# Shared pools, hand-ordered transposes and re-timed weight preparation between the mixer and the feed forward of a hybrid encoder layer

## The chip, the cores and the metric

The kernel runs on one core of one Trainium2 chip. The time is that of one execution on the device, in microseconds (us). A core has TensorE (PE, matrix products into PSUM), VectorE (DVE), ScalarE (ACT) and GpSimd (POOL) for elementwise work, and SyncE (SP), whose queue issues the transfers between DRAM and the on-chip memory SBUF.

## The reference

One layer (DEPTH = 1) over 2048 tokens of width 1024 in float32: windowed attention and a state space mixer in parallel, their outputs through w_out, then a feed forward of width 4096 with a squared relu.

```python
h = rms_norm(x, norm1[layer])
z = h @ w_in[layer]
...
att = windowed_gqa(q, k, v, q_gain[layer], k_gain[layer], sink[layer])
ssm = s5_mixer(u, lam_re[layer], ..., w_glu[layer])   # ends in gelu, then g_val * sigmoid(g_gate)
x = x + jnp.concatenate([att, ssm], axis=-1) @ w_out[layer]
h = rms_norm(x, norm2[layer])
x = x + jnp.square(jax.nn.relu(h @ w_ff1[layer])) @ w_ff2[layer]
```

## The kernel before

Every float32 number is split into an upper and a lower part of a format that TensorE takes, and each product is three matmuls (`mm3`, lines 85 to 89: upper by upper, upper by lower, lower by upper). So each operand needs a split: ScalarE copies the upper part, VectorE or GpSimd subtracts it for the lower part.

First come the input projection, the state space scan and attention (to about 680 us). What the change touches begins there.

The middle. `yprep` (line 836) loads the scan's output y in four quarters of tokens, four pieces each, applies the gelu and splits. `glu` (line 850) makes 96 matmuls per quarter into banks `pglu`, and the gate `sg` gives s in the tiles `sth` and `stl`. `load_split` brings the state space half of w_out in eight pieces through two buffers; GpSimd subtracts. `out_ssm` (line 1203) does per token tile of 128 two halves of 12 matmuls into `pos_` banks and VectorE adds x1 (the residual with attention's part, loaded from `x1_dr`). `norm2` (line 1228) takes the squares' sum on ScalarE, two scalar steps on VectorE, a power on GpSimd, and scales to h2 on VectorE.

The feed forward runs on 2 x 2 blocks with seven products instead of eight (PRODUCTS, numbered 1 to 7), so from each pair of token tiles seven operand pieces are made: four blocks b11, b21, b12, b22 and sums of them (t2, t3, t4 on GpSimd). They go to DRAM (`hc_dr`), are loaded back, transposed on TensorE (`trans`, banks `pth`), and split into `hb`. The tokens are done in two halves of 1024, tiles 0 to 7 first. For each half 16 blocks of `ff1_block` follow (32 in all, each 84 matmuls); a block's w1 is loaded two blocks ahead, summed (`left_w1`) and split (`split_w1`) one block ahead. The results f11, f12, f21, f22 and their sums s1 to s4 go to DRAM (`f_dr`). In block 16 the operands change to the second half of the tokens.

The second matrix runs over 8 chunks of w2 by 4 units of 256 tokens (32 units, each seven products of 12 matmuls). Each chunk's w2 is loaded as two pairs (`load_w2`), eight sums are made on VectorE (`right_w2`, lines 1460 to 1463) and 14 splits (`split_w2`); f pieces are loaded (`load_f`, four buffers) and split (`split_f`) a unit ahead. After each product VectorE adds the bank into `acc` (line 1541), which was loaded with x1.

A scheduler orders each engine's instructions from a model of when they are ready, so the order in the program is not that of the source; each engine then takes its own queue in order. Tiles are taken from pools; a pool that is opened where another one lay waits until that one's last use. With `tc.manual_schedule` an engine keeps the source's order.

## Time and profile before

| what | us |
|---|---|
| median of 3 runs | 2201.45 (2196.33 to 2203.27) |
| the profiled execution | 2200.2 |
| its span, first to last instruction | 2198.4 |
| TensorE busy | 2077.8 (95%) |
| VectorE, ScalarE, GpSimd busy | 67%, 46%, 27% |
| first matrix of the feed forward | about 907 to 1537 |
| second matrix | about 1553 to 2194 |

The page gives for each engine the time in which it worked. Where the engine that sets the time is busy nearly all along, one reads its idle time: when it lay, what released it, and at which clock it ran (the granted clock, as a share of the full rate).

### The profile page before, as it was taken

Reading aid. Unit: us, or ns where it says so; the run is one execution under the profiler, and the core shown is the slowest. Engines: PE = TensorE matmul, PEld = TensorE weight load, DVE = VectorE, ACT = ScalarE, POOL = GpSimd, SP = SyncE. Lnnn points to the kernel's source line nnn. Section 1 sums busy time; section 2 is a strip of 40 time slices with the busy share of each in tenths; the row PEclk is TensorE's granted clock in tenths of the full one; section 3 lists DMA queues with packets and bytes.
Section 4 is the critical chain, followed back from the end, with each engine's and each line's share of the span. In section 5 each row is a group of like instructions: output and inputs, shape, how many; then the busy total and the mean of one; then the engine's idle time right before and its main releaser. Section 6 shows DMA issues by size and latency. Waiting matters only on the chain.

```text
span 2198.4 us, 30479 instructions
## 1 busy us (share of the span) xinstructions
PE 2077.8 (95%) x10546; PEld 1706.7 (78%) x10546; DVE 1479.6 (67%) x2806; ACT 1016.0 (46%) x2061; POOL 590.3 (27%) x451
## 2 busy tenths in 40 slices
...
GB/s 252 292 82 159 157 125 142 108 100 117 96 125 160 163 153 279 224 149 152 153 158 176 203 156 146 146 151 99 255 212 101 129 128 98 134 130 114 112 135 162
DMA packets 284394, 337.06 MB, mean 153 GB/s; under 512 B 62928, under 2 KB 211408, under 8 KB 284240
## 3 DMA queue, kind: packets, MB, share of 16 engines
...
q8 instruction: 83, 1.36, 0.3%
q14 instruction: 71, 0.58, 0.1%
...
## 4 chain that ended last, share of the span: by engine, by line
PE 67%; DVE 13%; DMA 7%; POOL 5%; issue 3%; ACT 3%; SPq 1%; DVEq 0%; POOLq 0%; ACTq 0%
PE f L87 6%; PE f L89 6%; PE f L88 6%; PE f_al L89 5%; PE f_al L87 5%; PE f_al L88 5%; PE f_ga L87 3%; PE f_ga L89 3%; PE f_ga L88 3%; POOL w2s L1470 2%; PE pv L1075 1%; POOL fs L1496 1%; PE ptp L1065 1%; DVE acc L1541 1%; PE f_be L89 1%
## 5 line engine op out<-in xcount | busy, mean ns | idle before, releaser
L1541 DVE TENSOR_TENSOR acc<-f,acc 128x512 f32<-128x512 f32 x448 | 304.8, 687 | 164.6 <-PE f L89 158.0
L87 PE MATMUL f<-w2s,fs 128*128 128x512 f32 x896 | 352.9, 394 | 31.0 <-DVE acc L1541 15.7
L89 PE MATMUL f<-w2s,fs 128*128 128x512 f32 x896 | 351.4, 392 | 3.7 <-POOL fs L1496 3.7
L88 PE MATMUL f<-w2s,fs 128*128 128x512 f32 x896 | 351.3, 392 | 0.0
L1495 ACT ACTIVATE fs<-fr 128x512 fp32r<-128x512 f32 x224 | 141.6, 633 | 366.1 <-PE f L89 350.5
L1496 POOL TENSOR_TENSOR fs<-fr,fs 128x512 fp32r<-128x512 f32 x128 | 185.2, 1449 | 297.0 <-ACT fs L1495 255.8
L87 PEld LDWEIGHTS f<-w2s,fs 128*128 128x128 f32 x896 | 169.4, 189 | 74.1 <-ACT fs L1495 27.0
L1339 POOL TENSOR_TENSOR w1s<-w1r,w1s 128x512 fp32r<-128x512 f32 x96 | 135.2, 1409 | 311.9 <-ACT w1s L1338 303.0
L87 PE MATMUL f_al<-hb,w1s 128*128 128x512 f32 x512 | 201.0, 393 | 1.0 <-ACT w1s L1338 1.0
L89 PE MATMUL f_al<-hb,w1s 128*128 128x512 f32 x512 | 200.6, 392 | 1.1 <-DVE w1s L1339 0.9
L89 PEld LDWEIGHTS f<-w2s,fs 128*128 128x128 f32 x896 | 169.7, 189 | 40.3 <-POOL fs L1496 4.5
L88 PE MATMUL f_al<-hb,w1s 128*128 128x512 f32 x512 | 200.4, 391 | 0.0
L88 PEld LDWEIGHTS f<-w2s,fs 128*128 128x128 f32 x896 | 169.8, 190 | 34.7
L818 POOL TENSOR_TENSOR wgl<-wgr,wgh 128x512 fp32r<-128x512 f32 x8 | 10.4, 1311 | 521.0 <-DMA wgr<-in_w_glu_dram 508.2
L1339 DVE TENSOR_TENSOR w1s<-w1c,w1s 128x512 fp32r<-128x512 f32 x96 | 68.3, 711 | 88.0 <-ACT w1s L1338 88.0
L89 PEld LDWEIGHTS f_al<-hb,w1s 128*128 128x128 f32 x512 | 96.5, 189 | 22.0 <-DVE w1s L1339 1.3
L87 PEld LDWEIGHTS f_al<-hb,w1s 128*128 128x128 f32 x512 | 96.5, 189 | 21.3 <-ACT w1s L1338 1.4
L88 PEld LDWEIGHTS f_al<-hb,w1s 128*128 128x128 f32 x512 | 96.6, 189 | 19.6
L1338 ACT ACTIVATE w1s<-w1c 128x512 fp32r<-128x512 f32 x128 | 80.6, 630 | 49.7 <-PE f_al L89 48.4
L88 PE MATMUL f_ga<-hb,w1s 128*128 128x512 f32 x256 | 99.9, 390 | 0.0
L87 PE MATMUL f_ga<-hb,w1s 128*128 128x512 f32 x256 | 99.8, 390 | 0.0
L89 PE MATMUL f_ga<-hb,w1s 128*128 128x512 f32 x256 | 99.7, 389 | 0.0
...
## 6 DMA issues: line engine op xcount, KB each, us to landing
...
f_dr<-fs SPq DMA_DIRECT2D x128, 256.0 KB
...
```

What stands on the lines that cost most here:

```text
L87: nc.tensor.matmul(ps_ap, lhsT=lh, rhs=rh, start=first, stop=False, skip_group_check=onto)
L88: nc.tensor.matmul(ps_ap, lhsT=lh, rhs=rl, start=False, stop=False, skip_group_check=onto)
L89: nc.tensor.matmul(ps_ap, lhsT=ll, rhs=rh, start=False, stop=last, skip_group_check=onto)
L818: eng_lo.tensor_tensor(lo, raw, hi, op=ALU.subtract)
L1065: nc.tensor.transpose(pt[:, h, :], p[:, h, kt * P:(kt + 1) * P], ident)
L1075: nc.tensor.matmul(po[g * HD:(g + 1) * HD, :], lhsT=v_all[:, lo + kt, g * HD:(g + 1) * HD], rhs=pT.pop((n, g, kt)), start=kt == 0, stop=kt ...
L1338: ACT.activation(out=t[:, 0], in_=src, func=AF.Copy)
L1339: (DVE if m in (6, 7, 3) else POOL).tensor_tensor(t[:, 1], src, t[:, 0], op=SUB)
L1470: (DVE if m in (6, 7, 3) and fp else POOL).tensor_tensor(t[:, 1], src, t[:, 0], op=SUB)
L1495: ACT.activation(out=t[:, 0], in_=src, func=AF.Copy)
L1496: (DVE if m in (6, 7, 3) else POOL).tensor_tensor(t[:, 1], src, t[:, 0], op=SUB)
L1541: DVE.tensor_tensor(a[:, cs], po, a[:, cs], op=ADD)
```

## The change

Four things are changed.

1. One pool (`px0`, then `px`) stays open over both matrices of the feed forward. Its tiles `raw0` and `raw1` hold first s of the even quarters, then the raw w1 (both halves of a block in one tile), then the raw w2. Splits of w1, of w2 and of f share tags (`w0` to `w6`, pairs `fa` to `fd`, four `cp` cells). So the last ff1 block can prepare chunk 0 of w2 (loads, sums, 14 splits in part) and load four pieces of f. All small tiles are padded so that every tile begins at the same position modulo 256 bytes.
2. From token tile 8 to the first ff1 block TensorE's order is that of the source: `trans` reads h2, t2, t3, t4 directly from SBUF, two pieces after each half of `out_ssm`; tiles 8 to 15 don't pass through `hc_dr`. The first half of ff1 is now that of tiles 8 to 15; tiles 0 to 7 come through DRAM at the switch. t3 is now t2 - b11 (before: b22 less the old b12, GpSimd's), and from tile 8 on it is VectorE's.
3. The gelu of the next quarter and the loads of w_out are woven with the gate step by step, y pieces are loaded one ahead, and the first block's lower halves of w1 are all VectorE's, products 1 and 2 ahead of the sums.
4. In the second matrix each chunk's sums and splits stand at steps, one per product, instead of eight sums at two places. acc is not loaded: the first products of chunk 0 are copied into it by ScalarE (`FIRST_TO`), and x1 is added later by 32 additions on VectorE (`X_STEPS`, one buffer `x2`, tiles of w2's raw pair in the last chunk).

The core of the diff:

```diff
-    pos_stack, pn_stack, sb_stack = ExitStack(), ExitStack(), ExitStack()
+    pos_stack, pn_stack, px1_stack = ExitStack(), ExitStack(), ExitStack()
+
+    px0 = ctx.enter_context(tc.tile_pool(name="px0", bufs=1))
+    d1_stack, d1b_stack, pnb_stack = ExitStack(), ExitStack(), ExitStack()
     po_ = pos_stack.enter_context(tc.tile_pool(name="pos", bufs=1))
     wsh = po_.tile([P, 4, D], F32R, name="wsh")
     wsl = po_.tile([P, 4, D], F32R, name="wsl")
-    pn = pos_stack.enter_context(tc.tile_pool(name="pn", bufs=1))
-    g2 = pn.tile([P, D], F32, name="g2")
-    nc.sync.dma_start(out=g2, in_=norm2[0:1, :].to_broadcast([P, D]))
-    s_pools = [pos_stack.enter_context(tc.tile_pool(name="s1", bufs=1)),
-               sb_stack.enter_context(tc.tile_pool(name="s0", bufs=1))]
+    s_pool = pos_stack.enter_context(tc.tile_pool(name="s1", bufs=1))
...
+    def split_ws():
+        for half in range(2):
+            for k in range(4):
+                cs = slice(half * 512, half * 512 + 512)
+                load_split(pn, "x1", 2, w_out[0, AW + k * P:AW + (k + 1) * P, cs], wsh[:, k, cs], wsl[:, k, cs], POOL)
+                if k % 2:
+                    yield
...
-        pool = s_pools[(q + 1) % 2]
-        s_t[q] = tuple(pool.tile([P, 4, 512], F32R, tag=nm, name=nm) for nm in ("sth", "stl"))
+        pool, tags = (s_pool, ("sth", "stl")) if q % 2 else (px0, ("raw0", "raw1"))
+        s_t[q] = tuple(pool.tile([P, 4, 512], F32R, tag=tag, name=nm) for tag, nm in zip(tags, ("sth", "stl")))
...
-            junk = pn.tile([P, 512], F32, tag="junk", name="junk", bufs=1)
+            junk = ps.tile([P, 512], F32, tag="mm", name="junk")
...
-        POOL.tensor_tensor(t3, b22, b12, op=SUB)
-        POOL.tensor_tensor(b12, b12, b11, op=SUB)
-        POOL.tensor_tensor(t2, b22, b12, op=SUB)
+        first = n < NT // 2
+        if first:
+            for m, t in ((1, b11), (2, b21), (3, b22)):
+                nc.sync.dma_start(out=hc_dr[n // 2, m], in_=t)
+        eng = POOL if n < NT - 1 else DVE
+        eng.tensor_tensor(b12, b12, b11, op=SUB)
+        eng.tensor_tensor(t2, b22, b12, op=SUB)
+        (POOL if first else DVE).tensor_tensor(t3, t2, b11, op=SUB)
...
-    run(run_glu(0))
-    run(yprep(2), run_glu(1), out_quarter(0))
-    run(yprep(3), run_glu(2), out_quarter(1))
-    run(run_glu(3), out_quarter(2))
-    sb_stack.close()
+    weave(run_glu(0), yprep(1), split_ws())
+    weave(run_glu(1), yprep(2))
+    run(out_quarter(0))
+    weave(run_glu(2), yprep(3))
+    run(out_quarter(1))
+    pn_stack.close()
+    run(run_glu(3))
     glu_stack.close()
 
 
-    d1_stack = ExitStack()
+
     with tc.using_default_side("right"):
         pe = d1_stack.enter_context(tc.tile_pool(name="pe", bufs=1))
+        pn = pnb_stack.enter_context(tc.tile_pool(name="pnb", bufs=1))
+        px1 = px1_stack.enter_context(tc.tile_pool(name="px1", bufs=1))
+    g2 = load_gain(pn)
...
+    def raw_tile(i):
+        return px0.tile([P, 2, D], F32, tag=f"raw{i % 2}", name="wraw")
...
-    early = right_operands(0, [(m, i) for i in range(4) for m in PRODUCTS])
-    for n, _ in enumerate(out_quarter(3)):
-        if n > 0:
-            for _ in range(7):
-                next(early, None)
+    x1 = load_x1(NT // 2, px1, "x1", 2)
+
+    by_hand = ExitStack()
+    by_hand.enter_context(tc.manual_schedule(engines={mybir.EngineType.PE}))
+    queue = []
+    for n in range(NT // 2, NT):
+        nx = load_x1(n + 1, px1, "x1", 2) if n + 1 < NT else None
+        if n == NT - 1:
+            queue += [(m, 3, h2_t[n - 1][:, j * 512:j * 512 + 512]) for j, m in enumerate((1, 2))]
+        for _ in out_ssm(n, x1):
+            for _ in range(min(len(queue), 2 if n < NT - 1 else 3)):
+                trans(*queue.pop(0))
+        if n == 11:
+            load_w1(0)
+            load_w1(1)
+        nc.sync.dma_start(out=x1_dr[n * P:(n + 1) * P, :], in_=x1)
+        pend = norm2(n, x1)
+        if pend is not None and n < NT - 1:
+            queue += [(m, (n - NT // 2) // 2, pend[m]) for m in (1, 2, 3, 5, 6, 7, 4)]
+        x1 = nx
+    px1_stack.close()
     pos_stack.close()
...
+    px = ctx.enter_context(tc.tile_pool(name="px", bufs=1))
...
-        (DVE if m in (6, 7, 3) else POOL).tensor_tensor(t[:, 1], src, t[:, 0], op=SUB)
+        (DVE if m in (6, 7, 3) or g == 0 else POOL).tensor_tensor(t[:, 1], src, t[:, 0], op=SUB)
...
-        nc.sync.dma_start(out=f_dr[g % NFB, g // NFB, m], in_=t)
-
-    def cell(tag, bufs=1):
-        return pf.tile([P, 512], F32, tag=tag, name=tag, bufs=bufs)
+        nc.sync.dma_start(out=f_dr[g % NFB, 1 - g // NFB, m], in_=t)
...
+    def pair(tag):
+        t = px.tile([P, 2, 512], F32, tag=tag, name=tag)
+        return t[:, 0], t[:, 1]
...
-        f11 = cell("f11")
+        f11, f22 = pair("fa")
...
+    FS_PX = {1: "fa", 2: "fb", 7: "fc", 3: "fd"}
...
+    left_w1(0, (1, 2))
+    for m in (1, 2):
+        split_w1(0, m)
     left_w1(0)
...
+            k = PRODUCTS.index(m)
+            if k == 0:
+                right_w2(0, 0)
+            if k == 2:
+                right_w2(0, 1)
+            if k == 4:
+                load_f(0)
+                load_f(1)
+            if k == 5:
+                load_f(2)
+                load_f(3)
+                split_f(0)
+            for j in {1: (), 2: (1, 2)}.get(k, (k,)):
+                split_w2(0, j)
...
+    FIRST_TO = (1, 6, 5, 4)
...
+        steps = {3: load(0), 5: load(1)}
+        for fp in range(2):
+            for i, do in enumerate((sums, sum2, sum7, sum4)):
+                steps[11 + 4 * fp + i] = lambda do=do, fp=fp: do(fp)
+        for j in range(14):
+            steps[(14 if j < 4 else 17) + j, "split"] = lambda j=j: split_w2(c + 1, j)
+        return steps
...
+        for k in range(7):
+            if X_STEPS.get((u, k), (0, 1))[1] == 0:
+                n = X_STEPS[u, k][0]
+                if c < NC2 - 1:
+                    x2_t[n] = load_x1(n, p2, "x2", 1)
+                else:
+                    x2_t[n] = raw_tile(n)[:, 0]
+                    nc.sync.dma_start(out=x2_t[n], in_=x1_dr[n * P:(n + 1) * P, :])
...
-                DVE.tensor_tensor(a[:, cs], po, a[:, cs], op=ADD)
-            q = 7 * (u + 1) + k
-            split_f(q)
-            load_f(q + 4)
-            if more:
-                if u % 4 in (1, 2) and k == 3:
-                    right_w2(c + 1, u % 4 - 1)
-                if u % 4 == 3:
-                    for j in range(4 + 2 * k, min(6 + 2 * k, 14)):
-                        split_w2(c + 1, *W2_ORDER[j])
-                elif u % 4 == 2 and k > 2:
-                    split_w2(c + 1, *W2_ORDER[k - 3])
+                if c == 0 and m in FIRST_TO:
+                    ACT.copy(a[:, cs], po)
+                else:
+                    DVE.tensor_tensor(a[:, cs], po, a[:, cs], op=ADD)
+            if (u, k) in X_STEPS:
+                n, half = X_STEPS[u, k]
+                xs = slice(half * 512, half * 512 + 512)
+                DVE.tensor_tensor(acc[n][:, xs], acc[n][:, xs], x2_t[n][:, xs], op=ADD)
+            for q in F_STEPS[k] if u == 0 else (7 * (u + 1) + k,):
+                f_on(q)
+            if u == 0:
+                for j in W_STEPS.get(k, ()):
+                    split_w2(0, j)
+            step = 7 * (u % 4) + k
+            for do in (before.get((step + 28, "split")), plan.get(step), plan.get((step, "split"))):
+                if do is not None:
+                    do()
```

How the order moves, at three places. In the rows `[waits ...]` names the engines or queues whose signals the instruction waits for.

TensorE at the end of the middle, before; `pos_` is the out product of the last tile, `hs` a piece that comes from DRAM, `f_al` the first bank of ff1:

```order
L88 MATMUL pos__9407<-wsl,sth 128x512
L89 MATMUL pos__9407<-wsh,stl 128x512
L87 MATMUL pos__9407<-wsh,sth 128x512
L1292 MATMUL pth<-ident,hs 128x128 x4
L88 MATMUL pos__9407<-wsl,sth 128x512
L89 MATMUL pos__9407<-wsh,stl 128x512
L1292 MATMUL pth<-ident,hs 128x128 x72
L87 MATMUL f_al<-hb,w1s 128x512
```

After the change, in the last tile too; `t_9308`, `t_9307` and `t_9309` are t2, t3 and t4 of tiles 12 and 13 in SBUF:

```order
L92 MATMUL pos__9383<-wsh,sth 128x512
L93 MATMUL pos__9383<-wsl,sth 128x512
L94 MATMUL pos__9383<-wsh,stl 128x512
L1352 MATMUL pth<-ident,t_9308 128x128 x4
L1352 MATMUL pth<-ident,t_9307 128x128 x4
L1352 MATMUL pth<-ident,t_9309 128x128 x4
L92 MATMUL pos__9418<-wsh,sth 128x512
```

The 18 pieces that stood behind the last out product are now spread between the halves of the tiles, three here.

VectorE behind the last out product, before; L1294 is the lower half of a transposed piece, L1331 and L1329 are sums of w1, L1339 is the lower half of a product of w1:

```order
L1211 TENSOR_TENSOR x_9289<-pos__9407,x_9289 128x512 [waits PE_49]
L1235 TENSOR_TENSOR ss_9486<-ss_9486 128x1 [waits Activation_49]
L1236 TENSOR_SCALAR ss_9486<-ss_9486 128x1 [waits DVE_49]
L1238 SCALAR_TENSOR_TENSOR h_9485<-x_9289,ss_9486,g_7874 128x1024 [waits DMAHW1_49,DMAHW0_49,Pool_49]
L1294 TENSOR_TENSOR hb<-pth,hb 128x4x128 [waits Activation_49] x16
L1331 TENSOR_TENSOR w1c<-w1r 128x512 [waits DMAHW3_49,DMAHW2_49,DMAHW4_49,DMAHW1_49,DMAHW6_49,DMAHW0_49,DMAHW7_49,DVE_49,Pool_49]
L1294 TENSOR_TENSOR hb<-pth,hb 128x4x128 [waits Activation_49] x2
L1329 TENSOR_TENSOR w1c<-w1r 128x512 [waits DMAHW2_49]
L1339 TENSOR_TENSOR w1s<-w1c,w1s 128x512 [waits Activation_49]
L1330 TENSOR_TENSOR w1c<-w1c,w1r 128x512 [waits DVE_49]
```

After; L1354 is the lower half of a transposed piece, L1277 the scaling h2, L1290 to L1292 the sums of tiles 14 and 15, L1405 a sum of w1, L1415 a lower half of w1:

```order
L1248 TENSOR_TENSOR x_9314<-pos__9418,x_9314 128x512 [waits PE_49]
L1354 TENSOR_TENSOR hb<-pth,hb 128x4x128 [waits Activation_49] x2
L1274 TENSOR_TENSOR ss_9448<-ss_9448 128x1 [waits Activation_49]
L1275 TENSOR_SCALAR ss_9448<-ss_9448 128x1 [waits DVE_49]
L1277 SCALAR_TENSOR_TENSOR h_9447<-x_9314,ss_9448,g_8930 128x1024 [waits Pool_49]
L1290 TENSOR_TENSOR h_9447<-h_9447,h_9373 128x512 [waits DVE_49]
L1405 TENSOR_TENSOR wc<-wraw 128x512 [waits DMAHW5_49,DMAHW4_49]
L1291 TENSOR_TENSOR t_9458<-h_9447 128x512 [waits DVE_49]
L1415 TENSOR_TENSOR ws<-wraw,ws 128x512 [waits Activation_49]
L1292 TENSOR_TENSOR t_9457<-t_9458,h_9373 128x512 [waits DVE_49]
L1415 TENSOR_TENSOR ws<-wraw,ws 128x512 [waits Activation_49]
```

The lower halves of the first two products of w1 now stand between the sums of the last tile pair and ahead of the other sums of w1.

VectorE in the second matrix, at the turn of a chunk, before; L1541 adds a bank into acc, L1460 to L1463 are the sums of w2, L1496 is a lower half of f:

```order
L1496 TENSOR_TENSOR fs<-fr,fs 128x512 [waits DMAHW5_49,Activation_49]
L1460 TENSOR_TENSOR w2c<-w2r 128x512 [waits DMAHW6_49,DMAHW2_49,Pool_49]
L1541 TENSOR_TENSOR acc_15410<-f_16660,acc_15410 128x512 [waits PE_49]
L1461 TENSOR_TENSOR w2r<-w2r 128x512 [waits DVE_49]
L1541 TENSOR_TENSOR acc_15414<-f_16663,acc_15414 128x512 [waits PE_49]
L1496 TENSOR_TENSOR fs<-fr,fs 128x512 [waits DMAHW7_49,Activation_49]
L1541 TENSOR_TENSOR acc_15412<-f_16658,acc_15412 128x512 [waits PE_49]
L1462 TENSOR_TENSOR w2c<-w2r 128x512 [waits DVE_49]
L1541 TENSOR_TENSOR acc_15416<-f_16661,acc_15416 128x512 [waits PE_49]
L1463 TENSOR_TENSOR w2c<-w2r,w2c 128x512 [waits DVE_49,Pool_49]
L1541 TENSOR_TENSOR acc_14935<-f_16831,acc_14935 128x512 [waits PE_49]
```

After; L1736 adds into acc, L1660, L1667, L1672 and L1677 are the sums, L1558 is a lower half of f:

```order
L1558 TENSOR_TENSOR fs<-wc,fs 128x512 [waits DMAHW4_49,Activation_49]
L1660 TENSOR_TENSOR wraw<-wraw 128x512 [waits DMAHW7_49,Pool_49]
L1736 TENSOR_TENSOR acc<-f_16424,acc 128x512 [waits PE_49]
L1736 TENSOR_TENSOR acc<-f_16427,acc 128x512 [waits PE_49]
L1558 TENSOR_TENSOR fs<-wc,fs 128x512 [waits DMAHW5_49,Activation_49]
L1667 TENSOR_TENSOR wc<-wraw 128x512 [waits DMAHW1_49,DVE_49]
L1736 TENSOR_TENSOR acc<-f_16422,acc 128x512 [waits PE_49]
L1672 TENSOR_TENSOR wc<-wc,wraw 128x512 [waits DVE_49]
L1736 TENSOR_TENSOR acc<-f_16425,acc 128x512 [waits PE_49]
L1677 TENSOR_TENSOR wc<-wraw,wc 128x512 [waits Pool_49]
L1736 TENSOR_TENSOR acc<-f_16584,acc 128x512 [waits PE_49]
L1660 TENSOR_TENSOR wraw<-wraw 128x512 [waits DMAHW3_49]
```

The sum of b12 and b11 is now the first, the one that reads the second half of the raw tile comes two additions later, and behind them sums and additions alternate in both.

## Rows read from the trace of the kernel before

**Rows 1.** The page's part 1: engine, busy us (share of the span), number of instructions

```profile
PE 2077.8 (95%) x10546; PEld 1706.7 (78%) x10546; DVE 1479.6 (67%) x2806; ACT 1016.0 (46%) x2061; POOL 590.3 (27%) x451
```

**Rows 2.** Table by stretch: us, busy us of each engine, TensorE's clock, DMA share, GB/s

```profile
680.00:932.00 252.00, 223.37 (x958) 178.11 (x957) 140.52 (x196) 100.11 (x185) 73.97 (x63) 0.93 0.58 195
...
1240.00:1537.00 297.00, 297.00 (x1312) 245.93 (x1311) 146.53 (x208) 161.67 (x275) 79.62 (x59) 1.00 0.41 139
1537.00:1600.00 63.00, 39.15 (x141) 30.13 (x141) 44.71 (x49) 21.75 (x39) 35.65 (x25) 0.78 0.69 246
1600.00:2194.00 594.00, 583.14 (x2552) 477.28 (x2550) 424.71 (x588) 185.34 (x300) 283.42 (x192) 1.00 0.41 130
```

**Rows 3.** TensorE's waits, 680 to 932: for what, us in all, times, longest

```profile
PE pth L1292 <- DMA hs<-hc_dr: 12.1, 3, 6.7
...
PE pos__9119 L87 <- DVE x L1211: 3.9, 1, 3.9
PE pglu L87 <- ACT sg L862: 2.6, 1, 2.6
```

**Rows 4.** TensorE's timeline, 833 to 847: start, length, engine, line, operation, wait before

```profile
833.75 0.40 PE L88 MATMUL pos__9057<-wsl,sth 128*128 128x512 f32 x1
...
835.62 0.40 PE L87 MATMUL pos__9071<-wsh,sth 128*128 128x512 f32 x1
...
841.10 0.80 PE L87 MATMUL pos__9119<-wsh,sth 128*128 128x512 f32 x1 [3.92 <-DVE x L1211]
...
846.33 0.39 PE L87 MATMUL pos__9133<-wsh,sth 128*128 128x512 f32 x1
```

**Rows 5.** ScalarE's timeline, 699 to 710

```profile
699.09 0.63 ACT L817 ACTIVATE wsh<-x 128x512 fp32r<-128x512 f32 x1 [0.70 <-DMA x<-in_w_out_dram]
...
709.11 0.63 ACT L843 ACTIVATE y<-yr 128x512 f32<-128x512 f32 x1 [3.83 <-DMA yr<-y_dr]
```

**Rows 6.** VectorE's timeline around the scaling of a tile's norm

```profile
858.01 0.16 DVE L1235 TENSOR_TENSOR ss<-ss 128x1 f32<-128x1 f32 x1 [1.08 <-ACT junk L1234]
...
859.09 1.28 DVE L1238 SCALAR_TENSOR_TENSOR h<-x,ss,g 128x1024 f32<-128x1024 f32 x1 [0.73 <-POOL ss L1237]
```

**Rows 7.** GpSimd's timeline, one sum of transformed tokens

```profile
863.19 1.29 POOL L1251 TENSOR_TENSOR t<-h 128x512 f32<-128x512 f32 x1
```

**Rows 8.** TensorE's waits, 1537 to 2195

```profile
PE f L87 <- DVE acc L1541: 15.7, 15, 2.3
PE f L87 <- DMA fr<-f_dr: 15.3, 1, 15.3
PE f L89 <- POOL fs L1496: 3.7, 1, 3.7
```

**Rows 9.** TensorE's timeline at the boundary of the two matrices

```profile
1537.29 0.39 PE L89 MATMUL f_al<-hb,w1s 128*128 128x512 f32 x1
1552.92 0.80 PE L87 MATMUL f<-w2s,fs 128*128 128x512 f32 x1 [15.25 <-DMA fr<-f_dr]
```

**Rows 10.** VectorE's timeline in the second matrix

```profile
1643.73 0.87 DVE L1460 TENSOR_TENSOR w2c<-w2r 128x512 f32<-128x512 f32 x1 [2.09 <-POOL w2s L1470]
...
1645.12 1.18 DVE L1461 TENSOR_TENSOR w2r<-w2r 128x512 f32<-128x512 f32 x1
...
1657.01 0.68 DVE L1463 TENSOR_TENSOR w2c<-w2r,w2c 128x512 f32<-128x512 f32 x1
```

**Rows 11.** SyncE's queue, issue of one load of w2

```profile
1639.22 0.35 SPq L1453 DMA_DIRECT2D w2r<-in_w_ff_dram  x1
```

**Rows 12.** GpSimd's timeline before that load

```profile
1637.44 1.75 POOL L1470 TENSOR_TENSOR w2s<-w2r,w2s 128x512 fp32r<-128x512 f32 x1
```

**Rows 13.** TensorE's timeline, the stall after the sums

```profile
1652.16 0.47 PE L87 MATMUL f<-w2s,fs 128*128 128x512 f32 x1 [1.49 <-DVE acc L1541]
```

**Rows 14.** VectorE's timeline, the last s2 of the first matrix

```profile
1538.37 0.69 DVE L1394 TENSOR_TENSOR fs<-fs,f 128x512 f32<-128x512 f32 x1
```

**Rows 15.** Groups by line, GpSimd, 1600 to 2190: count, busy us, mean ns, idle before

```profile
L1496 POOL TENSOR_TENSOR fs<-fr,fs 128x512 fp32r<-128x512 f32 x118 | 171.0, 1451 | 289.1 <-ACT fs L1495 247.9 <-DVE acc L1541 41.2
```

314 lines of the change are left out of this document (200 added, 114 removed).

## The prediction

> **What bounds the kernel now.** I read the page's busy line first: TensorE is busy 2077.8 us of the 2198.4 us span [rows 1], so the change can only win what TensorE loses, and I looked for where that is. The table by stretch answers it [rows 2]. In the first feed forward matrix TensorE is busy 297.00 of 297 us at a granted clock of 1.00; nothing can be won there. Three stretches lose time. The middle, from attention's end to the first blocks of the feed forward (680 to 932), has 252 - 223.37 = 28.6 us idle, and its mean clock of 0.93 takes up to 0.07 x 252 = 17.6 us more: about 46. The boundary between the two feed forward matrices (1537 to 1600) has 23.9 us idle and a clock of 0.78, up to 13.9 more; since some of the slow clock falls into the idle time, I take 36. The second matrix (1600 to 2194) has 594 - 583.14 = 10.9 us idle at clock 1.00. Together about 93 us: the prize if every wait went and nothing came in its place. Then I asked the waits what ended these gaps. In the middle the longest are transposes that wait for pieces from DRAM (12.1 us), a sum that waits for x1 (3.9) and a gate (2.6) [rows 3]; at the boundary one wait of 15.3 us for the first f piece, one of 3.7 for POOL's split, the rest for VectorE's sums into acc [rows 8].
>
> **Middle: what goes, what comes.** The waits for DRAM pieces go: the transposes of tiles 8 to 15 read SBUF and stand between the two halves of each tile's product. The code gives no more transposes than before, and 28 loads and 28 stores of 256 KB less. I then walked through the new order with the old durations, and found these waits in it.
>
> First gate, quarter 0 to 1. The eight loads of w_out still go through two buffers, each held until POOL's split; the last lands at 699.09, and ScalarE then waited until 709.11 for the next y [rows 5]. In the new order ScalarE has the gelu of the last y piece of quarter 1 behind those splits, so it comes at about 710 to 711, while TensorE has used up quarter 0 and the pieces that are there at about 704. I put 6.7 us of idle plus 1.8 of slow clock: 8.5 (3 to 10).
>
> Tile 8. Its x1 and gain tiles lie in the place of the gate's pool, so their loads go out only after quarter 3's gate. In the trace a late x1 load made TensorE wait 3.92 us, and the 12 matmuls behind it took 846.33 - 841.10 = 5.2 us; at the spacing before it (835.62 - 833.75 = 1.87 us for 8, so 0.234 each) they would take 2.8 [rows 4]. So 3.9 + 2.4 = 6.3; I take 7, since here a gain load of the same size stands in the same queue (2 to 10).
>
> Tiles 9 to 13. The sum t3 is now VectorE's and waits for POOL's t2, which stands behind POOL's b12; each is about 1.3 us [rows 7], and two copies of transposed pieces are queued behind t3 on VectorE. TensorE needs their bank: 2 x 1.3 less 0.3 of other work, three times: 7 (0 to 9).
>
> Block 0. Behind tile 15 VectorE has, in a row, the two scalar steps, the scaling h2, then L1290, L1405, L1291, and only then the lower half of w1's first product. Scalar steps to the end of h2: 858.01 to 859.09 + 1.28 = 2.4 us, after 1.08 of waiting for the squares [rows 6]: 3.4; with four instructions at about 0.69 the half is there 6.2 us after the last sum, about 7 after the last product. TensorE has eight transposes (1 us), a wait for their copy (1.3) and two matmuls; the third needs that half: 4.3 idle, and about 2 of slow clock as in [rows 4]. With small change after it: 9 (6 to 11).
>
> Boundaries between quarters and leftovers: 3. Sum 8.5 + 7 + 7 + 9 + 3 = 34.5 against 46: **-12** (0 to -25).
>
> **Boundary of the two matrices.** The shared pool lets w2's loads, sums and first splits and four f loads run under the last ff1 block. What cannot move ahead of it: the first f split goes into the pair "fa", which f11 and f22 hold until the block's last s2 has read them. In the trace TensorE's last matmul starts at 1537.29 and the next at 1552.92 [rows 9]; s2 is done at 1538.37 + 0.69 = 1539.06 [rows 14], 1.4 us after TensorE's end. Then ScalarE's split and POOL's 1.45 us (mean of 118) [rows 15]: the first lower half is there about 3.5 to 4.5 us after the end, POOL's next some 3 us later. So 4.4 of idle and 2.5 of slow clock: 7 (5 to 12) in place of 36: **-29** (-24 to -31). The cover for w2's loads is the block's 19 us of matmuls; were it not enough, each missing load would cost the 4.5 us below.
>
> **The second matrix: the spread sums.** The stall that returns with every chunk of w2 is read at 1652.16: 1.49 us [rows 13]. VectorE's eight sums alternate with the additions into acc, 1.18 + 0.69 per addition, while TensorE brings one each 1.36 us, and it started late: the first sum at 1643.73 after 2.09 us of waiting [rows 10]. The page names POOL, but the load that the sum reads left at 1639.22 [rows 11], when POOL's split of the old half ended (1637.44 + 1.75 = 1639.19) [rows 12]; 4.5 us later it was there. In the new program's source the sums lie one per product, but in VectorE's order they still alternate with the additions, at the same place in the chunk, and the first half of the raw tile now waits for the same POOL split, because both halves are one tile. So I leave the 10.9. x1 is no longer loaded into acc: 32 additions of acc and x2 come to VectorE, at 0.68 where POOL rests and 1.18 where it runs [rows 10], 22 to 38 us in 594 us where VectorE had 424.71 busy [rows 2]: hidden, but two of them come with their load not yet there (one buffer, 4.5 us): +2 (-11 to +8). The acc copies of chunk 0 by ScalarE (185 of 594 us busy) cost nothing.
>
> The trace agrees with a rule of the Trainium skill here (GPSIMD Engine Reference, Specifications), by which POOL shares its SBUF interfaces with VectorE and contends with VectorE instructions that have two SBUF inputs. It speaks against the 32 additions: by it all 32 would be at 1.18, 38 us instead of 22, and the sum above would not change, since VectorE has 169 us free.
>
> **Pool positions.** All tiles now share one alignment. The out product's spacing of 0.234 [rows 4] could become ff1's 297/1312 = 0.226 [rows 2]: 16 tiles of 24 matmuls x 0.008 = 3. I take **-2** (0 to -5).
>
> **Sum.** -12 - 29 + 2 - 2 = -41. The profiled execution took 2200.2 us (span 2198.4), 1.2 under the median of 2201.45: 2200.2 - 41 = **2159**.
>
> **Rivals.**
> 1. Every wait goes as laid out (w2's sums spread in time, tiles 8 to 15 without a stop): middle 10 left, boundary 3, chunks 0: -36 - 33 - 11 - 2 = -82, so 2118. For it: the parts are there. Against it: VectorE's order of sums, which hardly changed. Chance 0.13.
> 2. The middle wins nothing: waits for t3, x1 and block 0 cost the 46 again. -29 + 2 - 2 = -29, 2171, up to 2180 if tiles 8 to 15 stop oftener than I count. For it: three engines in a tight chain, and an order of TensorE that cannot step past a wait. Chance 0.22.
> 3. Clock. After each stop in tiles 8 to 15 TensorE runs on at the lower of its levels for the whole tile. Eight tiles of 24 matmuls at 0.227 = 5.4 us would take twice that: +43, so 2202. Against it: 12 matmuls after the 3.92 us stop the spacing was back, and the 1.49 us stop of [rows 13] stands in a stretch of clock 1.00. Chance 0.04. The Trainium skill (TensorE: Matmul & The Clock Gate, HAM oscillation) tells of a kernel whose waits between groups put the clock down at every group; by that rule the time would be this rival's.
> 4. Slower: the single x2 buffer. Each of 16 loads can leave only when the last addition from that buffer is done, and VectorE, which takes its queue in order, stands at the next one for the whole 4.5 us [rows 10 to 12] with the sums into acc behind it and TensorE without a bank. 16 x 4.5 = 72: 2159 + 72 = 2231. It decides from 41/16 = 2.6 us each. Against it: in the order four additions of acc or more, 5.4 us of TensorE's pace, lie between most of these. Chance 0.05.
>
> **How the numbers follow.** Forecast, 2146 to 2169: 0.50. Rival 1 0.13, rival 2 0.22, rival 3 0.04, rival 4 0.05, and 0.06 between the forecast and rival 1. About 0.3% (6.6 us) is what a measurement can tell from no change: faster 0.91, same 0.04, slower 0.05. The range reaches over rival 2 with its upper end and stops short of rival 1: 2132 to 2182 leaves out most of rival 1, and rivals 3 and 4.
>
> **What would show it.** In the new trace: the stretch from attention's end to ff1 12 us shorter, with waits of about 4 us at tile 9 and before ff1's third matmul; no wait for hc pieces before the switch; the boundary with one stop of about 4 us; stalls of 1 to 2 us still at every chunk, on acc. Wrong would be: chunks without stalls (the sums did spread), or single waits over 8 us in tiles 8 to 15.

## The result, and the profile after

| | us |
|---|---|
| before, median of 4 runs | 2200.44 (2196.33 to 2203.27) |
| after, median of 4 runs | 2166.2 (2163.06 to 2169.0) |
| ratio after to before | 0.9847, 95% interval 0.983 to 0.9864 |
| the profiled execution after, its span | 2169.0, 2167.2 |

The kernel became 34 us faster, where the prediction said 41. The profile that follows is that of the slowest of the four executions after; from trace to trace the difference is 31.1 us in the last matmul's start. Here is where they lie. Each line is the distance between two starts of matmuls that can be read in the timelines, so the lines add up.

| stretch | before | after | difference |
|---|---|---|---|
| start to attention's last matmul | 680.40 | 682.91 | +2.5 |
| middle, to ff1's first matmul | 226.6 | 205.9 | -20.7 |
| first matrix, to its last matmul | 630.3 | 635.1 | +4.8 |
| boundary and second matrix, to the last matmul | 656.3 | 638.5 | -17.8 |

The middle and the first matrix must be taken together (-15.9), since transposes that stood ahead of ff1 before stand now in its first block. The first line is not a loss: in the eleven further kernels below, none of which changes anything ahead of it but unalign, it lay between 679.9 and 684.6.

The page's part 1 of the changed kernel, which answers to [rows 1]:

```profile
PE 2070.1 (96%) x10546; PEld 1704.2 (79%) x10546; DVE 1490.5 (69%) x2816; ACT 1027.7 (47%) x2093; POOL 578.9 (27%) x441
```

TensorE has the same 10546 matmuls and is busy 7.7 us less; the other 23.5 us of the span's 31.2 were idle time. The table by stretch (columns as in [rows 2]) shows what is left of it:

```profile
680.00:764.00 84.00, 80.67 (x343) 64.78 (x342) 51.06 (x66) 40.34 (x69) 22.93 (x19) 0.98 0.52 161
764.00:850.00 86.00, 80.96 (x356) 64.70 (x354) 48.27 (x69) 31.02 (x61) 21.78 (x20) 0.98 0.44 154
850.00:920.00 70.00, 60.60 (x287) 48.07 (x288) 50.56 (x79) 32.64 (x67) 20.81 (x17) 0.95 0.38 130
...
1500.00:1560.00 60.00, 54.56 (x229) 44.30 (x228) 39.10 (x44) 36.92 (x65) 36.30 (x25) 0.94 0.59 197
...
1680.00:2160.00 480.00, 470.52 (x2054) 384.91 (x2053) 361.66 (x499) 147.19 (x242) 230.19 (x155) 1.00 0.43 139
```

Idle time in the middle fell from 28.6 us to 17.8 in the first three lines (84 - 80.67, 86 - 80.96, 70 - 60.60), and the clock is 0.95 to 0.98 there instead of 0.93. From token tile 8 to the end of tile 15, with its many short stops, it is the full one:

```profile
821.00:884.00 63.00, 57.16 (x286) 45.40 (x285) 38.09 (x63) 23.42 (x54) 16.95 (x16) 1.00 0.43 152
```

Around the boundary of the matrices 5.4 us are idle at 0.94 where [rows 2] had 23.9 at 0.78. In the rest of the second matrix 9.5 us are idle, about as before.

TensorE's waits from 600 to 2170: for what, us in all, times, longest. They answer to [rows 3] and [rows 8].

```profile
PE f L92 <- DVE acc L1736: 10.9, 8, 3.9
PE pth L1352 <- DVE hb L1354: 5.3, 8, 1.2
PE f L92 <- ACT fs L1557: 5.2, 4, 2.8
...
PE pth L1352 <- DMA hs<-hc_dr: 2.6, 2, 1.4
PE pos__8646 L92 <- DVE x L1248: 2.5, 1, 2.5
```

The 15.3 us on an f piece from DRAM and the 12.1 on transposed pieces are gone; what is left of `hs` comes at the switch between the halves of the tokens. New are the stop of 4.6 us on the first product of w1 and two of 2.8 and 2.7 us on the first splits of f. The sums into acc, 15.7 us in 15 stops before, are 10.9 in 8.

TensorE's timeline at the boundary, which answers to [rows 9], and at the turn of the first chunk ([rows 13]): start, length, engine, line, operation, wait before.

```profile
1523.96 0.39 PE L94 MATMUL f_al<-hb,ws 128*128 128x512 f32 x1
1527.11 0.50 PE L92 MATMUL f<-ws,fs 128*128 128x512 f32 x1 [2.76 <-ACT fs L1557]
...
1530.75 0.80 PE L94 MATMUL f<-ws,fs 128*128 128x512 f32 x1 [2.68 <-POOL fs L1558]
...
1618.43 0.79 PE L92 MATMUL f<-ws,fs 128*128 128x512 f32 x1 [3.90 <-DVE acc L1736]
```

The upper half of the first f split is there 3.1 us after the last matmul's start. As the prediction had it, it follows the last s2 (L1473): s2 is done at 1526.22, and ScalarE's split starts at 1526.44. GpSimd's lower half comes 3.6 us later than the upper one. The prediction had it 3.5 to 4.5 us after TensorE's end; it is there 6.3 us after it (1530.69, the end of the first L1558, against 1524.35), since two splits of w2 (L1532) stand ahead of it in GpSimd's queue. GpSimd's timeline:

```profile
1525.58 3.45 POOL L1532 TENSOR_TENSOR ws<-wraw,ws 128x512 fp32r<-128x512 f32 x2 [4.63 <-ACT ws L1531]
1528.98 3.40 POOL L1558 TENSOR_TENSOR fs<-wc,fs 128x512 fp32r<-128x512 f32 x2
```

The third stop, 3.90 us, is longer than any on acc before. VectorE's timeline ahead of it:

```profile
1611.88 0.69 DVE L1667 TENSOR_TENSOR wc<-wraw 128x512 f32<-128x512 f32 x1 [1.85 <-DMA wraw<-in_w_ff_dram]
1612.61 1.81 DVE L1672 TENSOR_TENSOR wc<-wc,wraw 128x512 f32<-128x512 f32 x1
1614.34 1.76 DVE L1677 TENSOR_TENSOR wc<-wraw,wc 128x512 f32<-128x512 f32 x1
1616.03 1.75 DVE L1660 TENSOR_TENSOR wraw<-wraw 128x512 f32<-128x512 f32 x1
1617.70 1.28 DVE L1736 TENSOR_TENSOR acc<-f,acc 128x512 f32<-128x512 f32 x2
```

Four sums of w2 stand in a row, behind 1.85 us of waiting for the load of w2, with no addition into acc between them, and three of them take 1.75 to 1.81 us instead of 0.69. From 1609.4, the end of the addition before, to 1617.70 VectorE frees no bank; ScalarE copies one out, at 1612.40.

### The profile page after: what moved, and what is told of

Same layout as the page of the kernel before. It is cut to its first block, busy times and chain, and to the rows that moved or that the text cites. A ratio compares the mean times of both kernels' runs of the same rounds, so it can differ in the third digit from the quotient of the medians.

```text
span 2167.2 us, 30329 instructions
## 1 busy us (share of the span) xinstructions
PE 2070.1 (96%) x10546; PEld 1704.2 (79%) x10546; DVE 1490.5 (69%) x2816; ACT 1027.7 (47%) x2093; POOL 578.9 (27%) x441
## 4 chain that ended last, share of the span: by engine, by line
PE 70%; DVE 12%; DMA 6%; POOL 4%; ACT 3%; issue 3%; SPq 1%; POOLq 0%; DVEq 0%; ACTq 0%
PE f L92 7%; PE f L94 7%; PE f L93 7%; PE f_al L94 5%; PE f_al L93 5%; PE f_al L92 5%; PE f_ga L94 3%; PE f_ga L92 3%; PE f_ga L93 3%; POOL ws L1532 2%; PE pv L1094 1%; POOL fs L1558 1%; PE f_be L92 1%; PE f_be L93 1%; PE f_be L94 1%
## 5 line engine op out<-in xcount | busy, mean ns | idle before, releaser
L1736 DVE TENSOR_TENSOR acc<-f,acc 128x512 f32<-128x512 f32 x416 | 281.0, 686 | 138.8 <-PE f L94 138.7
L92 PE MATMUL f<-ws,fs 128*128 128x512 f32 x896 | 352.4, 393 | 16.1 <-DVE acc L1736 10.9
L94 PE MATMUL f<-ws,fs 128*128 128x512 f32 x896 | 351.3, 392 | 2.7 <-POOL fs L1558 2.7
L93 PE MATMUL f<-ws,fs 128*128 128x512 f32 x896 | 350.7, 391 | 0.0
L1557 ACT ACTIVATE fs<-wc 128x512 fp32r<-128x512 f32 x224 | 140.7, 631 | 313.3 <-PE f L94 292.4
L1558 POOL TENSOR_TENSOR fs<-wc,fs 128x512 fp32r<-128x512 f32 x128 | 186.4, 1458 | 288.6 <-ACT fs L1557 254.3
L92 PEld LDWEIGHTS f<-ws,fs 128*128 128x128 f32 x896 | 169.5, 189 | 57.8 <-ACT fs L1557 8.6
L1415 POOL TENSOR_TENSOR ws<-wraw,ws 128x512 fp32r<-128x512 f32 x93 | 131.5, 1415 | 286.2 <-ACT ws L1414 282.8
L92 PE MATMUL f_al<-hb,ws 128*128 128x512 f32 x512 | 201.2, 393 | 4.6 <-ACT ws L1414 4.6
L93 PE MATMUL f_al<-hb,ws 128*128 128x512 f32 x512 | 200.7, 392 | 0.8 <-DVE hb L1354 0.8
L94 PE MATMUL f_al<-hb,ws 128*128 128x512 f32 x512 | 200.6, 392 | 0.6 <-DVE ws L1415 0.6
L94 PEld LDWEIGHTS f<-ws,fs 128*128 128x128 f32 x896 | 169.5, 189 | 38.6 <-POOL fs L1558 3.1
L93 PEld LDWEIGHTS f<-ws,fs 128*128 128x128 f32 x896 | 169.7, 189 | 35.0
L1415 DVE TENSOR_TENSOR ws<-wc,ws 128x512 fp32r<-128x512 f32 x97 | 66.5, 688 | 84.8 <-ACT ws L1414 84.8
L92 PEld LDWEIGHTS f_al<-hb,ws 128*128 128x128 f32 x512 | 96.7, 189 | 24.8 <-ACT ws L1414 4.8
L94 PEld LDWEIGHTS f_al<-hb,ws 128*128 128x128 f32 x512 | 96.7, 189 | 21.1 <-DVE ws L1415 1.3
L93 PEld LDWEIGHTS f_al<-hb,ws 128*128 128x128 f32 x512 | 96.7, 189 | 20.7 <-DVE hb L1354 1.2
L1414 ACT ACTIVATE ws<-wc 128x512 fp32r<-128x512 f32 x128 | 80.6, 630 | 53.0 <-PE f_al L94 48.1
L92 PE MATMUL f_ga<-hb,ws 128*128 128x512 f32 x256 | 100.0, 391 | 0.0
L94 PE MATMUL f_ga<-hb,ws 128*128 128x512 f32 x256 | 99.7, 390 | 0.0
L93 PE MATMUL f_ga<-hb,ws 128*128 128x512 f32 x256 | 99.7, 389 | 0.0
```

The costliest lines, as they stand in the source:

```text
L92: nc.tensor.matmul(ps_ap, lhsT=lh, rhs=rh, start=first, stop=False, skip_group_check=onto)
L93: nc.tensor.matmul(ps_ap, lhsT=lh, rhs=rl, start=False, stop=False, skip_group_check=onto)
L94: nc.tensor.matmul(ps_ap, lhsT=ll, rhs=rh, start=False, stop=last, skip_group_check=onto)
L1414: ACT.activation(out=t[:, 0], in_=src, func=AF.Copy)
L1415: (DVE if m in (6, 7, 3) or g == 0 else POOL).tensor_tensor(t[:, 1], src, t[:, 0], op=SUB)
L1557: ACT.activation(out=t[:, 0], in_=src, func=AF.Copy)
```

## The experiments

All ratios are to the kernel before, run in the same session; the changed kernel's is 0.9847. Times are medians of 4 or 5 runs. "Boundary" is the time from ff1's last matmul to about the 350th matmul behind it, less 0.2267 us for each of these: 31.4 us before, 8.6 after. "Middle" and "second matrix" are the lines of the table above. In the kernels that change nothing there the middle lay between 205.6 and 209.0 us, one trace each, so a difference of 3 us in it is not a finding.

### VectorE's order in the second matrix: dve_hand

```diff
     f_on(2)
+    ctx.enter_context(tc.manual_schedule(engines={mybir.EngineType.DVE}))
     plan, before = {}, {}
```

> The changed kernel with VectorE's order in the second matrix taken from the source: its eight sums of w2 now stand one per product, two or three additions into acc apart, and the 32 additions of x1 where the steps put them. Theory A (the stalls at the chunk turns come from where the scheduler puts the sums: next to the reload of w2, which waits for GpSimd's last split): the 3.90 us stall at the first turn with its slow clock (about 6 us) and the 9.5 us at the later turns go to 3 or less: 2152 to 2157 us against 2166. Theory B (VectorE is too full there in any order, since each of its sums takes 1.18 us while GpSimd runs): the stalls move and stay about 15 us: 2163 to 2170. Theory C (an order by hand makes VectorE stand at splits whose upper half is late): slower, above 2172.

Measured: 2147.62 us (2147.05 to 2153.24), ratio 0.978 (0.9759 to 0.9801). The second matrix, from ff1's last matmul on, takes 618.6 us instead of 638.5. TensorE's waits there from 1530 on, whole (one of 2.24 us on the first f split lies before, at 1528.82):

```profile
PE f L92 <- ACT acc L1735: 1.8, 1, 1.8
PE f L94 <- POOL fs L1558: 1.1, 1, 1.1
PE f L92 <- DVE acc L1737: 0.6, 1, 0.6
```

From chunk to chunk TensorE no longer stops, but for 0.6 us. Theory A's reason holds; the gain, 14.7 us by the two ratios ((0.9847 - 0.978) x 2200), is at the far end of its 9 to 14. VectorE's additions into acc and sums by line, 1700 to 2160, first of the changed kernel (count, busy us, mean ns, idle before), then, 1700 to 2150, of dve_hand:

```profile
L1736 DVE TENSOR_TENSOR acc<-f,acc 128x512 f32<-128x512 f32 x331 | 223.6, 687 | 99.9 <-PE f L94 99.8
...
L1672 DVE TENSOR_TENSOR wc<-wc,wraw 128x512 f32<-128x512 f32 x9 | 11.1, 1228 | 0.0
L1677 DVE TENSOR_TENSOR wc<-wraw,wc 128x512 f32<-128x512 f32 x9 | 10.6, 1176 | 0.0
L1660 DVE TENSOR_TENSOR wraw<-wraw 128x512 f32<-128x512 f32 x8 | 9.4, 1181 | 4.6 <-DMA wraw<-in_w_ff_dram 3.3 <-POOL ws L1532 1.2
```

```profile
L1737 DVE TENSOR_TENSOR acc<-f,acc 128x512 f32<-128x512 f32 x330 | 224.0, 687 | 95.1 <-PE f L94 92.6
...
L1667 DVE TENSOR_TENSOR wc<-wraw 128x512 f32<-128x512 f32 x10 | 6.9, 685 | 0.0
L1660 DVE TENSOR_TENSOR wraw<-wraw 128x512 f32<-128x512 f32 x10 | 6.8, 684 | 0.0
L1677 DVE TENSOR_TENSOR wc<-wraw,wc 128x512 f32<-128x512 f32 x10 | 6.8, 684 | 0.0
L1672 DVE TENSOR_TENSOR wc<-wc,wraw 128x512 f32<-128x512 f32 x10 | 6.8, 682 | 0.0
```

The plan that the source writes out, one sum per product, was right; the scheduler did not keep it on VectorE. Where it is kept, the sums also no longer wait for a load (idle 0.0 in all four rows of sums, 4.6 us in the row of L1660 above, 3.3 of it for the load) and take 0.68 us instead of 1.18 to 1.23. The Trainium skill (GPSIMD Engine Reference, Specifications) says that GpSimd's SBUF interfaces are shared with VectorE for instructions with two SBUF inputs. These rows agree with that: the sums read two SBUF tiles and differ between the kernels, while the additions into acc, which read one operand from PSUM, keep a mean of 687 ns in both.

What the order changes is who starts first. In the changed kernel 47 of the 56 sums (L1660 to L1677) start while a GpSimd instruction is at work, and 45 of these end 0.54 to 0.56 us after it, so they last as long as it still runs and 0.55 us more. In dve_hand none of the 56 does. There 25 are followed by a GpSimd instruction 0.08 to 0.16 us after their start and still take 0.68; it is the GpSimd instruction that is longer then, about 1.68 us. GpSimd and VectorE in the changed kernel, then in dve_hand:

```profile
1612.58 1.29 POOL L1532 TENSOR_TENSOR ws<-wraw,ws 128x512 fp32r<-128x512 f32 x1 [3.19 <-ACT ws L1531]
1612.61 1.81 DVE L1672 TENSOR_TENSOR wc<-wc,wraw 128x512 f32<-128x512 f32 x1
```

```profile
1649.18 0.68 DVE L1672 TENSOR_TENSOR wc<-wc,wraw 128x512 f32<-128x512 f32 x1
1649.34 1.68 POOL L1558 TENSOR_TENSOR fs<-wc,fs 128x512 fp32r<-128x512 f32 x1 [6.48 <-ACT fs L1557]
```

### The sums put back to two places: group

```diff
-            step = 7 * (u % 4) + k
-            for do in (before.get((step + 28, "split")), plan.get(step), plan.get((step, "split"))):
-                if do is not None:
-                    do()
+            if c + 1 < NC2:
+                if k == 0 and u % 4 < 2:
+                    load_w2(c + 1, u % 4)
+                if u % 4 in (1, 2) and k == 3:
+                    right_w2(c + 1, u % 4 - 1)
...
```

> The changed kernel with the eight sums and the splits of each chunk back at the places in the source where the kernel before had them (two groups, in the middle of two units), all else as changed; the scheduler still orders. Theory A (the spread in the source does nothing, since the scheduler places the sums as early as they can go): the same stalls at the turns, 2163 to 2169 us. Rival (the spread is what shortened the later turns from 10.9 to 9.5 and more): 2172 or more.

Measured: 2164.63 us (2162.76 to 2168.9), ratio 0.9852 (0.9829 to 0.9876): no difference, as theory A had it. VectorE's order of sums and additions is practically that of the changed kernel, and the stops on acc are 9.4 us in 9 places. So spreading the sums in the source alone did nothing; the scheduler put them into the same order from either source.

### acc loaded, no copies, no later additions of x1: acc_load

```diff
-    FIRST_TO = (1, 6, 5, 4)
+    FIRST_TO = ()
...
-    for c in range(1, NC2):
+    for c in range(0):
...
-                    acc[j] = p2.tile([P, D], F32, tag=f"acc{j}", name="acc")
+                    acc[j] = load_x1(j, p2, f"acc{j}", 1)
```

> The changed kernel with acc loaded with x1 in chunk 0 as before, no copies by ScalarE and no 32 additions later. Theory A (the first chunk turn costs 6 instead of 2 us because four sums stand there in a row with no addition between them, and the additions of x1 add a little): first turn back to about 2 us, later turns as they are, boundary about 9 to 11: 2160 to 2165. Rival (loading x1 into acc at the boundary, 16 loads of 512 KB, is what cost time before): boundary 13 or more, 2168 to 2175.

Measured: 2165.56 us (2163.05 to 2166.62), ratio 0.9851 (0.9824 to 0.9877). The time is the same, but its parts are not. TensorE's timeline, boundary and first chunk:

```profile
1528.66 0.79 PE L94 MATMUL f<-ws,fs 128*128 128x512 f32 x1 [2.69 <-POOL fs L1558]
...
1563.20 0.50 PE L92 MATMUL f<-ws,fs 128*128 128x512 f32 x1 [2.85 <-DVE acc L1736]
```

The boundary lost 12.1 us instead of 8.6, by a new stop on acc at 1563.20: ahead of it VectorE has seven sums of w2 in a row, from 1551.0 to 1562.5. The stop at the first turn shrank from 3.90 to 1.89, and with the slow clock behind it the turn lost 3.5 us instead of 5.7; there the sums alternate with additions. So neither theory held alone. ScalarE's copies, with acc not loaded, give 3.6 us up to the first turn and cost 2.2 at it. After that the changed kernel loses 14.9 us and this one 12.9, so the 32 additions cost 2 us at most, which the times don't show.

### The first chunk of w2 prepared later, without and with a pool of its own: no_prep, two_pools

no_prep takes the preparation out of the last ff1 block and writes it down behind it; two_pools does this and also closes the two shared pools, px0 and px, and opens them again for the second matrix.

```diff
-            if k == 0:
-                right_w2(0, 0)
-            if k == 2:
-                right_w2(0, 1)
...
+    load_w2(0, 0)
+    load_w2(0, 1)
+    for q in range(4):
+        load_f(q)
+    right_w2(0, 0)
...
```

two_pools alone:

```diff
     d1_stack.close()
+    px_stack.close()
+    px0_stack.close()
+    px0 = ctx.enter_context(tc.tile_pool(name="px0", bufs=1))
+    px = ctx.enter_context(tc.tile_pool(name="px", bufs=1))
```

> The changed kernel without preparation of the second matrix under the last block of the first: w2's chunk 0 is loaded, summed and split, and the first f pieces are loaded, after that block. Theory A (the 23 us won at the boundary come from that preparation): boundary 25 to 32 us instead of 8.7, 2182 to 2190. Rival (the gain comes from the shared pool, which lets loads leave without waiting for the pool of the first matrix to close, so loads leave early anyway): boundary 12 to 18, 2169 to 2176.

> As no_prep, and the two shared pools are closed with the first matrix and opened again in the same places for the second, so a tile of the second matrix waits for the last use of what lay there. Theory A (it is the pool that stays open that lets the preparation run under the last block, wherever it stands in the source; the boundary was 8.7 us with it and 31.5 before): boundary 22 to 32 us, 2178 to 2190 us. Rival (the boundary is short because acc is no longer loaded and the first products go to ScalarE): boundary 9 to 14, 2164 to 2170.

Measured: no_prep 2164.6 us (2162.04 to 2167.12), ratio 0.9849 (0.9827 to 0.9872), boundary 8.3, shorter than either expectation had it. The place in the source does not matter: from 1530 us on VectorE's order is the changed kernel's, instruction by instruction, since the scheduler moves the preparation ahead as soon as its tiles have a place. That is the rival's reason, with more effect than it was given. two_pools 2180.96 us (2179.18 to 2184.01), ratio 0.9928 (0.9914 to 0.9941), boundary 22.0, at the lower edge of theory A. TensorE's timeline there:

```profile
1532.74 0.79 PE L92 MATMUL f<-ws,fs 128*128 128x512 f32 x1 [9.23 <-DMA wc<-f_dr]
...
1540.10 0.80 PE L94 MATMUL f<-ws,fs 128*128 128x512 f32 x1 [6.14 <-POOL fs L1559]
```

The wait for an f piece from DRAM is back. 22.0 - 8.3 = 13.7 us of the boundary hang on the pool that stays open, and the times differ by 16.4. Of the 31.4 - 22.0 = 9.4 us that two_pools still gains at the boundary, acc_load puts 3.6 to ScalarE's copies; the rest was not taken apart.

### Alignment undone: unalign

```diff
-    cst.tile([P, 24], F32, name="offset")
...
-        return pool.tile([rows, 64], F32, **kw)[:, 0:n]
+        return pool.tile([rows, n], F32, **kw)
```

> The changed kernel with the small tiles at their own sizes again and without the tile that shifts all others, so tiles begin at different positions modulo 256 bytes, as before. Theory A (only the out product's spacing depends on it): spacing of its matmuls back from 0.227 to 0.234 us, 2.4 us in all, 2166 to 2171. Rival (the front's spacings depend on it too): 2171 to 2176. Third: no difference in any spacing, 2163 to 2168.

Measured: 2182.06 us (2178.21 to 2187.74), ratio 0.9933 (0.9915 to 0.9951): 16 us slower than the changed kernel, where 10 at most were expected. Two stretches inside the first matrix, TensorE without an idle moment in both: first the changed kernel, then unalign (columns as in [rows 2]).

```profile
940.00:1180.00 240.00, 240.00 (x1060) 198.80 (x1059) 124.32 (x177) 132.98 (x228) 68.48 (x50) 1.00 0.45 152
```

```profile
950.00:1180.00 230.00, 230.00 (x987) 184.75 (x987) 116.68 (x166) 125.32 (x213) 63.07 (x47) 1.00 0.43 148
```

At the same clock the starts of the matmuls are 0.2267 us apart in the one and 0.2333 in the other. The first matrix takes 651.5 us instead of 635.1. So the expectation was right that position counts, and wrong about which tiles it would hit. It is w1's or the tokens' tiles, for the 2688 matmuls of the first matrix. The out product keeps its spacing: without stops and slow clock its matmuls start 0.2288 us apart here, 0.2282 in the changed kernel and 0.2334 in the kernel before. What it won came with the new pools, padded or not. In the kernel before ff1's tiles happened to lie well (297 us for 1312, 0.226, [rows 2]); with the new pools they need the padding to do so.

### TensorE's order left to the scheduler: no_hand

```diff
     by_hand = ExitStack()
-    by_hand.enter_context(tc.manual_schedule(engines={mybir.EngineType.PE}))
     queue = []
```

> The changed kernel without the order by hand on TensorE from tile 8 to the first block; the transposes still read SBUF and the scheduler places them. Theory A (the gain of the middle is that the pieces no longer come from DRAM; the order by hand adds little): 2163 to 2172 us, the stretch from attention's last product to ff1's first within 4 us of 205.9. Rival (the order by hand carries it, since the scheduler bunches the transposes behind the last tile, as before): stretch longer by 8 to 15, 2174 to 2181.

Measured: 2160.96 us (2160.24 to 2164.06), ratio 0.9838 (0.9824 to 0.9851). The middle takes 201.2 us instead of 205.9. The intervals of the two ratios overlap, so that it is faster is not shown by the times; that the order by hand does not carry the gain of the middle is. That is theory A's reason; time and middle lie just under its ranges. No run sends the pieces of tiles 8 to 15 through DRAM again or undoes the weaving of the gate, so what the middle gained is read from the waits that went and not from an experiment.

### t3 on GpSimd: t3_pool

```diff
-        (POOL if first else DVE).tensor_tensor(t3, t2, b11, op=SUB)
+        (POOL if n < NT - 1 else DVE).tensor_tensor(t3, t2, b11, op=SUB)
```

> The changed kernel with the sum t3 of tiles 9 to 13 on GpSimd, behind t2, instead of on VectorE. Theory A (the prediction's): t3 on VectorE waits for GpSimd's t2 and the transposed pieces behind it wait with it, so the waits of TensorE on the copies (0.57, 0.85, 0.85 and 1.21 us) go: 2 to 4 us less, about 2163. Theory B: GpSimd's chain of b12, t2, t3 and t4 grows by 1.3 us per pair and the last transposes come later by that much: no change or up to 3 us more, 2166 to 2169.

Measured: 2163.73 us (2159.94 to 2164.97), ratio 0.9832 (0.9816 to 0.9848); the middle takes 203.9 us. TensorE's waits on the copies of transposed pieces, 675 to 960, first in the changed kernel and then here:

```profile
PE pth L1352 <- DVE hb L1354: 3.5, 4, 1.2
```

```profile
PE pth L1352 <- DVE hb L1354: 1.3, 1, 1.3
```

As theory A expected, three of four stops go; the 2.2 us are below what the times and the middle can tell (the intervals overlap).

### The parts that helped, together: best1, no_hand_dve, no_hand_dve_w

best1 is dve_hand, and the split of w1's first product lies in the pool that is open early; no_hand_dve is dve_hand and no_hand; no_hand_dve_w has all three. The edit that the others don't show:

```diff
-        t = split_tile(f"w{PRODUCTS.index(m)}").rearrange("p a (k f) -> p a k f", k=4)
+        i = PRODUCTS.index(m)
+        t = split_tile(f"w{i}", px0 if i < NW0 else px).rearrange("p a (k f) -> p a k f", k=4)
```

> dve_hand with one more edit: the split of w1's first product gets its place in the pool that is open from the middle on, so it need not wait for the x1 tiles to be free; its two halves can be made before the last tile's end. Theory A (in block 0 TensorE's 4.56 us stood for that place: ScalarE's split waited for the scaling that reads x1): the first product runs 4 us earlier, and product 2's halves, which come behind the sums of the last tiles, then set the pace: 2 to 4 us less than dve_hand, 2144 to 2146. Rival (VectorE's row of sums behind the last tile sets block 0 in any case): 2147 to 2149.

> The source of the changed kernel, with the scheduler ordering TensorE's work from tile 8 on and VectorE's order that of the source in the second matrix. Theory A, the two gains lie in different stretches and add: about 5 us from the middle (no_hand) and 18.6 from the second matrix (dve_hand), so 2166.2 - 23.6 = 2143, from 2140 to 2147. Theory B, the part that the scheduler wins in the middle is given back at the start of the second matrix, because the scheduler then places the preparation of the first chunk of w2 otherwise when it does not order VectorE there: as dve_hand alone, 2147 to 2151.

> As no_hand_dve, and the split of the first of w1's seven products lies in the pool that is open from attention's end, so that its upper half need not wait for the pool that opens where x1 lay. Theory A: at the first block the stop of 4.56 us (upper half) shrinks to the wait for the last pieces of the tokens, 3 us and some of the slow clock with it: 2 to 4 us under no_hand_dve, about 2140. Theory B: without the order by hand TensorE already has other work there and the stop is hidden: the same as no_hand_dve within 1.5 us.

| kernel | us | ratio | middle | second matrix |
|---|---|---|---|---|
| dve_hand | 2147.62 | 0.978 (0.9759 to 0.9801) | 208.7 | 618.6 |
| best1 | 2147.94 (2145.7 to 2153.02) | 0.9777 (0.9761 to 0.9793) | 201.9 | 619.5 |
| no_hand_dve | 2147.3 (2145.49 to 2148.8) | 0.976 (0.9745 to 0.9774) | 202.6 | 620.2 |
| no_hand_dve_w | 2144.61 (2143.23 to 2150.98) | 0.9748 (0.9733 to 0.9763) | 202.7 | 621.4 |

best1 lies in its rival's range: the stop of 4.56 us is 0.25 in its trace, but stops on the second product (0.80 and 1.09 us) come in its place, and the time is that of dve_hand. In no_hand_dve both stretches keep their gains, so the mechanism of theory A holds, while its time lies at the border of the two (2147): dve_hand's own gain is the 14.7 us by the ratios, not the 18.6 by which its median lay under that of after. In no_hand_dve_w the stop of 4.56 us on w1's first product is gone; TensorE's timeline at the first block:

```profile
887.33 0.50 PE L92 MATMUL f_al<-hb,ws 128*128 128x512 f32 x1 [0.25 <-ACT hb L1353]
...
891.63 0.50 PE L92 MATMUL f_be<-hb,ws 128*128 128x512 f32 x1 [0.79 <-ACT ws L1415]
...
897.51 0.73 PE L92 MATMUL f_al<-hb,ws 128*128 128x512 f32 x2 [1.15 <-ACT ws L1415]
```

It waits in smaller portions for the next splits instead, and in this trace no stretch is shorter than in no_hand_dve. Its median is 2.7 us lower, within the overlap of the intervals. It has the lowest median of this study, 2.5% under the kernel before and about 1% under the changed one (0.9748 against 0.9847, intervals apart).

## Why the prediction was right, and where it was off

The forecast, 2146 to 2169, holds the median of 2166.2, and its mechanism holds in all three parts; that of the middle is read from the waits, the other two were tried. Of the rivals none came: the clock is 1.00 from tile 8 to tile 15 (rival 3); the x2 buffer cost nothing that the time shows (rival 4, acc_load); the middle gained (rival 2); the waits did not all go (rival 1). Against the sum of -41 stand -31 from trace to trace and -34 by the medians. Term by term:

**Middle, -12, and pool positions, -2: right in sum (-15.9 measured), its parts mixed.** The loss can be counted as at the boundary. From attention's last matmul to the end of ff1's second block stand 917 matmuls and 112 transposes before (680.40 to 948.92), 920 and 112 after (682.91 to 933.90). At 0.2267 and 0.109 us each, their spacings where nothing waits, that is 220.1 and 220.8 us. So 48.4 us were lost before, 2.7 of it by the out product's wider spacing, and the 46 put down was right. After, 30.2 are lost where the terms below add up to 34.5. Of the 18.2 between them 0.7 go on the three more matmuls and 1.7 are lost again at the switch between the halves of the tokens.

- First gate, 8.5 put down: 705.25 waits 2.69 us, later stops there 0.22 and 0.42; with the slow clock 5.8 us are lost from 702 to 714. The y piece came earlier than I had laid out.

```profile
705.25 0.50 PE L92 MATMUL pglu<-yh,wgh 128*128 128x512 f32 x1 [2.69 <-ACT yh L866]
```

- Tile 8, 7 put down: two stops of 0.78, 2.2 us lost from 826 to 836. The step that failed is that the loads could leave only after quarter 3's gate: SyncE issued them at 816.41 and 816.80, some 5 us before that gate's last matmul and 11 ahead of the first of these stops. The addition that this stop waits for starts at 825.12 without a wait for its load, right behind the gate's last lower half on VectorE. SyncE's queue, and then TensorE:

```profile
816.41 0.34 SPq L1201 DMA_DIRECT2D g<-in_norm_dram  x1
816.80 0.42 SPq L1236 DMA_DIRECT2D x<-x_dr  x1
```

```profile
827.77 0.50 PE L92 MATMUL pos__8979<-wsh,sth 128*128 128x512 f32 x1 [0.78 <-DVE x L1248]
```

- t3, 7 put down: 3.5 in four stops, 7.0 lost from 836 to 884 with two stops on x and the changes between matmuls and transposes. VectorE did stand at t3 for GpSimd's sum, 2.11 us here, and t3_pool shows that the stops hang on it:

```profile
840.18 0.69 DVE L1292 TENSOR_TENSOR t<-t,h 128x512 f32<-128x512 f32 x1 [2.11 <-POOL t L1291]
```

- Block 0, 9 put down: 4.56 + 0.60 + 0.77 of stops and slow clock up to 894.6, 9.5 lost from 884 to 934. The size is right, the first cause was another. I had the lower half of w1's product late; the upper was, too:

```profile
888.17 1.67 ACT L1414 ACTIVATE ws<-wraw 128x512 fp32r<-128x512 f32 x3 [2.58 <-DVE h L1277]
...
888.85 0.79 PE L92 MATMUL f_al<-hb,ws 128*128 128x512 f32 x1 [4.56 <-ACT ws L1414]
...
890.67 0.80 PE L94 MATMUL f_al<-hb,ws 128*128 128x512 f32 x1 [0.60 <-DVE ws L1415]
```

ScalarE's split waits for h2's scaling, which does not feed it: the pool `px` lies where the tiles of x1 lay, and that scaling is the last to read x1. best1 and no_hand_dve_w, with that one tile elsewhere, have 0.25 us in its place, where dve_hand and no_hand_dve have 4.6. This is a wait for a place, which I saw at the boundary and overlooked here.

- Pool positions: the out product's matmuls now come each 0.227 us (840.35 - 839.67 = 0.68 for 3), 0.234 before [rows 4]. The size of -2 is right, but unalign shows that it is not the common alignment that gives it.

```profile
839.67 0.39 PE L93 MATMUL pos__9057<-wsl,sth 128*128 128x512 f32 x1
...
840.35 0.39 PE L93 MATMUL pos__9057<-wsl,sth 128*128 128x512 f32 x1
```

- Leftovers, 3 put down: 2.5 in one stop, on `pos__8646`, 5.7 lost in all that lies between the stretches above.

So the first gate and tile 8 were too dear by 7.5 us, the leftovers too cheap by 2.7. That the sum came so near is in part luck.

**Boundary, -29: -22.8 measured.** What remains, 8.6, was near the 7 put down, in two stops of 5.4 us together instead of one of 4.4. The term that was mis-sized is what the kernel before lost: I had added 23.9 of idle and a slow clock to 36, and by the count of matmuls it was 31.4. The mechanism is shown by two_pools: with the pool closed in between the waits return, 13.7 us at the boundary.

**Second matrix, +2: +5 measured** (20.6 us lost over 2328 matmuls, 15.6 before), inside the bounds of -11 to +8. Right was that the sums would not spread (group) and that the additions of x1 are hidden (acc_load); from 1700 to 2160 they took 0.87 to 0.88 us in the mean, between the 0.68 and 1.18 put down. Wrong was the sentence that ScalarE's copies cost nothing: with additions taken from VectorE's queue four sums came to stand in a row at the first turn, a stop of 3.90 us, 5.7 with the slow clock behind it; without the copies it is 1.89, 3.5 in all. The turns after it kept a stop on acc each, as forecast, of 0.33 to 1.95 us. dve_hand shows what stood behind both numbers, VectorE's order.

**What is left open.** In dve_hand the sums are spread over the products, don't wait for their loads and no longer start beside a GpSimd instruction at work; how much of its gain each of these has was not separated. Nor was the middle's gain divided among the pieces that stay in SBUF, the weaving and the new order of the tokens' halves.
